# Two decay masks moved from PSUM to the factors they multiply, and block-diagonal gates packed onto four quarters of TensorE

## The chip, the cores and the metric

The kernel runs on one core of a Trainium2 chip. The metric is the device time of one execution in microseconds (us). A core has five engines with a queue each: TensorE (PE, with its weight loads shown apart as PEld), VectorE (DVE), ScalarE (ACT), GpSimd (POOL) and SyncE (SP), which issues nearly all transfers. Each engine works through its queue in order and waits, at an instruction, for what that instruction needs.

## What is computed

Two layers run over 256 positions of width 1024. The first has a Mamba-2 mixer, a gated linear recurrence (RG-LRU) and a gated feed-forward part; the second has four branches, one of them a gated delta net. The change touches three places of this:

```python
# first layer, SSD: decay between positions l >= s of a chunk, per head
seg   = a_cs[..., :, None] - a_cs[..., None, :]
decay = exp(where(causal, seg, -inf))
cb    = einsum("bclgn,bcsgn->bgcls", cc, bc)
y_diag = einsum("bgcls,bgecls,bcsgep->bclgep", cb, decay, xdt)

# first layer, RG-LRU: 16 blocks of 64 channels, two gates
xc = causal_dwconv(u_x, conv_w, conv_b)
xb = xc.reshape(b, s, 16, 64)
r = sigmoid(einsum("bshi,hij->bshj", xb, wr) + br)
i = sigmoid(einsum("bshi,hij->bshj", xb, wi) + bi)

# second layer, delta net: decay of a chunk, per head
L    = where(strict, (kb @ k.T) * exp(where(strict, diff, 0)), 0)
a_qk = where(incl,   (q  @ k.T) * exp(where(incl,   diff, 0)), 0)
```

## The kernel before

The large products (projections) set the length of the program. A weight is loaded in halves of 128 x 1024 numbers (`wraw`, three buffers, transfers on SP's queue), rounded by ACT (L112, `whi`) and its remainder taken by DVE (L113, `wlo`), five buffers each. A projection is three products of rounded parts, 128-row weights against 256 or 512 columns of positions. `z0` to `z3` and `lx0` to `lx3` are made by `proj_wide` (L468, then an ACT copy L471 and a DVE sum L472), the gates `g0` to `g3` and the outputs `pa`, `pb` of the two mixers by L430 to L432.

Everything else of a layer is written as generators beside the main loop: `side_ssd`, `side_lru`, `side_gn` (the norm of the SSD's output, which makes `YAH`, `YAL`, the input of `pa`), `side_decay`, `side_delta`. At each stop of a projection the main loop runs one of them up to its next `yield`, and so PE's order is fixed by where these stops fall. The queues of ACT, DVE, POOL and SP are put in order by a scheduler from estimated times.

**SSD.** During `z` and `lx`, `decay(h)` makes, for each of 16 heads, a PSUM tile `pe` of 384 columns: the running sum `csT` of the head broadcast over the rows (L719), and on its first 256 columns a large negative number above the diagonal, added by a product of the identity with `low2r` (L721). Three Exp on ACT (L723, L725, L726) give `M`, DVE multiplies it by the block products `CB` (L727). After every second head PE multiplies `M` by `XD` (`py`, L737); PE's queue holds `py` of heads 2t and 2t+1 ahead of the projection that goes on.

**RG-LRU.** `lx` of a pair p goes through a convolution over positions (ACT L607, then three DVE steps L610 for each of two tiles) into `XC`. `side_lru` then takes one 128-channel tile after another, eight in all: two float32 products of a 128 x 128 block-diagonal weight (two 64 x 64 blocks, zeros beside them) with 256 columns, one per gate, both in one PSUM bank `pg`, and two Sigmoids on ACT (L789, L790). The weights `lw` are 1 MB.

**Delta net.** `side_decay` makes per chunk c a bank `pdE` of 4 heads x 128 columns: the mask product (L1189, 512 columns), four broadcasts of the running sum (L1192), four Exp (L1196). DVE multiplies the result `EE` into the products `pkk` (L1295, L1300).

Of the kernel before, what the change touches and what calls it, by code (L numbers as in the profile page):

```python
# [11 lines left out]
ALU = mybir.AluOpType  # L12
# [184 lines left out]
def two_blocks_kernel(  # L197
# [113 lines left out]
    low2r = cp.tile([P, 2 * P], F32R, name="low2r")  # L311
# [7 lines left out]
    def constants():  # L319
# [22 lines left out]

        for i in range(2):
            nc.vector.tensor_scalar(low2r[:, i * P : (i + 1) * P], triu, -NEG, NEG,
                                    op0=ALU.mult, op1=ALU.add)
# [42 lines left out]
    def rows(o, src, nm, wait):  # L388

# [11 lines left out]
        w = o.shape[1] - S  # L401
        nc.vector.tensor_copy(o[:, w : w + S], pT[:, 0:S])
        if w:
            nc.vector.tensor_copy(o[:, 0:P], pT[:, P:S])
# [250 lines left out]
    lw = big.tile([P, 2, 8, P], F32, tag="lw", name="lw")  # L655
# [6 lines left out]
    csT = sm.tile([P, 384], F32R, name="csT", bufs=1)  # L662
    ncs = sm.tile([P, 32], F32, name="ncs", bufs=1)
    ncb = sm.tile([P, 16], F32, name="ncb", bufs=1)

    def side_dt():
# [19 lines left out]
        nc.vector.tensor_scalar(ncs, cs[:, 0:32], -1.0, None, op0=ALU.mult)  # L686
# [15 lines left out]
    def side_ssd():  # L702

        yield ("bc", 9)
        for g in range(2):
# [6 lines left out]
            nc.vector.tensor_copy(CB[:, g, :], pb[:, 0:384])  # L712
            yield 1
# [62 lines left out]
    GY = act8("b8", "GY")  # L776
    LA = act8("b5", "LA")
# [1109 lines left out]
```

## Time and profile before

| | before |
|---|---|
| median of 3 runs | 826.16 us (826.12 to 826.82) |
| the profiled execution's own time | 825.72 us |
| its span in the profile | 824.0 us |
| PE busy | 809.6 us (98%) |
| DVE busy | 612.2 us (74%) |
| ACT busy | 524.6 us (64%) |
| POOL busy | 61.0 us (7%) |

The span is the time between the first and the last instruction that the profiler recorded; 1.7 us of the execution lie outside it. A busy share is a mean over the whole program: PE is full nearly everywhere, ACT is full in some stretches and idle in others.

### The profile page before, as it was taken

Reading aid. Unit: us, or ns where it says so; the run is one execution under the profiler, and the core shown is the slowest. Engines: PE = TensorE matmul, PEld = TensorE weight load, DVE = VectorE, ACT = ScalarE, POOL = GpSimd, SP = SyncE. Lnnn points to the kernel's source line nnn. Section 1 sums busy time; section 2 is a strip of 40 time slices with the busy share of each in tenths; the row PEclk is TensorE's granted clock in tenths of the full one; section 3 lists DMA queues with packets and bytes.
Section 4 is the critical chain, followed back from the end, with each engine's and each line's share of the span. In section 5 each row is a group of like instructions: output and inputs, shape, how many; then the busy total and the mean of one; then the engine's idle time right before and its main releaser. Section 6 shows DMA issues by size and latency. Waiting matters only on the chain.

```text
span 824.0 us, 13302 instructions
## 1 busy us (share of the span) xinstructions
PE 809.6 (98%) x5060; PEld 721.0 (87%) x5060; DVE 612.2 (74%) x1026; ACT 524.6 (64%) x820; POOL 61.0 (7%) x101
## 2 busy tenths in 40 slices
PE   6999999999999999999999999999999999999997
PEld 6999888888889999999988889888888888888886
DVE  5989789889689788888744697877786647566583
ACT  7575988895656666565643478956976555544452
POOL 0000000000110000000000100028830000000000
PEclk9999999999999999999999999999999999999999
DMA  8545435556754655555555544542454344555551
GB/s 310 204 172 212 153 104 207 177 205 201 257 186 149 216 189 185 182 177 191 201 196 193 192 158 151 182 157 104 169 156 149 130 143 167 202 190 192 190 193 52
DMA packets 41248, 147.12 MB, mean 179 GB/s; under 512 B 4896, under 2 KB 5152, under 8 KB 41056
## 3 DMA queue, kind: packets, MB, share of 16 engines
q1 hardware_dynamic: 40464, 145.35, 51.1%
q0 software_dynamic: 576, 0.92, 0.5%
q8 instruction: 40, 0.66, 0.3%
q14 instruction: 24, 0.20, 0.1%
q10 hardware_dynamic: 144, 0.00, 0.0%
HBM read 144.94 MB, written 1.31 MB: 177 GB/s over the span
## 4 chain that ended last, share of the span: by engine, by line
PE 92%; DVE 5%; ACT 1%; DMA 1%; issue 1%; DVEq 0%; SPq 0%; ACTq 0%
PE z L468 8%; PE fu L432 6%; PE fu L431 6%; PE fu L430 6%; PE g L430 5%; PE g L432 5%; PE g L431 5%; PE lx L468 3%; PE fd L431 3%; PE fd L432 3%; PE fd L430 3%; PE up L430 2%; PE up L431 2%; PE up L432 2%; PE o L432 2%; PE o L430 2%
## 5 line engine op out<-in xcount | busy, mean ns | idle before, releaser
L113 DVE TENSOR_TENSOR wlo<-wraw,whi 128x1024 fp32r<-128x1024 f32 x256 | 311.9, 1226 | 131.6 <-ACT whi L112 130.1
L112 ACT CAST whi<-wraw 128x1024 fp32r<-128x1024 f32 x256 | 266.3, 1049 | 198.4 <-PE fu L431 48.0
L430 PE MATMUL fu<-HX,whi 128*128 128x256 f32 x384 | 108.7, 283 | 0.0
L431 PE MATMUL fu<-HX,whi 128*128 128x256 f32 x384 | 108.7, 283 | 0.0
L432 PE MATMUL fu<-HX,wlo 128*128 128x256 f32 x384 | 108.7, 283 | 0.0
L430 PE MATMUL g<-whi,HX 128*128 128x512 f32 x192 | 76.7, 399 | 0.0
L432 PE MATMUL g<-whi,HX 128*128 128x512 f32 x192 | 74.9, 390 | 0.0
L431 PE MATMUL g<-wlo,HX 128*128 128x512 f32 x192 | 74.8, 390 | 0.0
L430 PEld LDWEIGHTS fu<-HX,whi 128*128 128x128 f32 x384 | 73.7, 192 | 0.0
L431 PEld LDWEIGHTS fu<-HX,whi 128*128 128x128 f32 x384 | 73.7, 192 | 0.0
L432 PEld LDWEIGHTS fu<-HX,wlo 128*128 128x128 f32 x384 | 73.7, 192 | 0.0
L468 PE MATMUL z<-HX,whi 128*128 128x512 f32 x192 | 70.1, 402 | 0.0
L468 PE MATMUL z<-HX,wlo 128*128 128x256 f32 x192 | 51.0, 286 | 0.0
L610 DVE SCALAR_TENSOR_TENSOR fc<-fu,pc,fc 128x255 f32<-128x255 f32 (+1 forms) x96 | 43.8, 478 | 1.6
L432 PEld LDWEIGHTS g<-whi,HX 128*128 128x128 f32 x192 | 36.0, 188 | 7.7
L431 PEld LDWEIGHTS g<-wlo,HX 128*128 128x128 f32 x192 | 36.1, 188 | 7.2
L430 PEld LDWEIGHTS g<-whi,HX 128*128 128x128 f32 x192 | 36.1, 188 | 7.2
L431 PE MATMUL fd<-wlo,FH 128*128 128x512 f32 (+1 forms) x120 | 41.7, 347 | 0.0
L430 PE MATMUL fd<-whi,FH 128*128 128x512 f32 (+1 forms) x120 | 41.6, 347 | 0.0
L432 PE MATMUL fd<-whi,FL 128*128 128x512 f32 (+1 forms) x120 | 41.6, 347 | 0.0
L468 PEld LDWEIGHTS z<-HX,whi 128*128 128x128 f32 x192 | 35.5, 188 | 6.8 <-issue 0.9
L468 PEld LDWEIGHTS z<-HX,wlo 128*128 128x128 f32 x192 | 36.2, 189 | 1.5
(539 smaller groups left out, 1922.7 us busy)
## 6 DMA issues: line engine op xcount, KB each, us to landing
wraw<-in_w_in_dram SPq DMA_DIRECT2D x130, 512.0 KB, 3.8
wraw<-in_w_fu_dram SPq DMA_DIRECT2D x48, 512.0 KB, 3.8
wraw<-in_w_fd_dram SPq DMA_DIRECT2D x24, 512.0 KB, 3.7
wraw<-in_w_o_dram SPq DMA_DIRECT2D x16, 512.0 KB, 3.5
wraw<-in_w_up_dram SPq DMA_DIRECT2D x16, 512.0 KB, 3.4
wraw<-in_w_pa_dram SPq DMA_DIRECT2D x8, 512.0 KB, 3.6
wraw<-in_w_pb_dram SPq DMA_DIRECT2D x8, 512.0 KB, 4.4
wraw<-in_w_mk_dram SPq DMA_DIRECT2D x4, 512.0 KB, 4.1
```

The source lines that it names most:

```text
L112: nc.scalar.copy(hi, raw)
L113: nc.vector.tensor_tensor(out=lo, in0=raw, in1=hi.bitcast(F32), op=ALU.subtract)
L430: nc.tensor.matmul(o, wh, xh, start=first, stop=False)
L431: nc.tensor.matmul(o, wh, xl, start=False, stop=False)
L432: nc.tensor.matmul(o, wl, xh, start=False, stop=last)
L468: nc.tensor.matmul(*p, start=k + i == 0, stop=k == 7 and i == 1)
L610: nc.vector.scalar_tensor_tensor(o[:, d:S], in0=p[:, 0 : S - d], scalar=col(wname, (taps - 1 - d) * n + i), in1=o[:, d:S], op0=ALU.mult, o ...
```

## The change

1. **SSD decay.** `pe` keeps only the broadcast running sum, 256 columns wide (`csT` is 256 wide instead of 384), and the mask product and `low2r` are gone. On ACT, two Relu of 128 columns give max(cs - csT, 0), that is minus the decay's exponent where it is allowed and zero above the diagonal; one Exp over 256 columns of `M` itself follows, and the third Exp reads `pe` as before. What stands above the diagonal is now a finite number, and POOL sets the same places of `CB` to zero, once per group (`affine_select`).
2. **LRU gates.** Two tiles (a pair p) are taken at once. Eight products with 64 rows and 64 columns of weights: gate r uses `XC`, with block 0 on rows and columns 0 to 63 and block 1 on 64 to 127; gate i uses `XW`, a copy of `XC` with its two halves of 64 partitions swapped, on the two other quarters. Gate r has one PSUM bank for both tiles and gate i another. `XW` is filled by two transfers per pair of 64 partitions x 512 numbers (128 KB), issued on POOL's queue after the convolution's last step; the gates wait for them. `lw` is 512 KB, there are four stops of `side_lru` instead of eight, and each comes at the sixth tick after its `lx` event instead of the fifth.
3. **Delta net decay.** The mask product is gone; four Relu and one Exp of 512 columns take the place of four Exp, and POOL zeroes `EE` above the diagonal before DVE reads it.

```diff
-            nc.tensor.matmul(pe[:, 0:384], sel16[:, h : h + 1].to_broadcast([P, P]), csT,
-                             start=True, stop=False)
-            nc.tensor.matmul(pe[:, 0:256], identr, low2r, start=False, stop=True)
+            nc.tensor.matmul(pe[:, 0:S], sel16[:, h : h + 1].to_broadcast([P, P]), csT,
+                             start=True, stop=True)
             M = tmp(f"M{h}", 384, tag="pt", bufs=4)
-            nc.scalar.activation(
-                M[:, 0:128], pe[:, 0:128], AF.Exp, bias=ncs[:, 16 + h : 17 + h])
-            nc.scalar.activation(M[:, 128:256], pe[:, 128:256], AF.Exp, bias=ncs[:, h : h + 1])
-            nc.scalar.activation(M[:, 256:384], pe[:, 256:384], AF.Exp, bias=ncb[:, h : h + 1])
+            for b in range(2):
+                nc.scalar.activation(M[:, (1 - b) * P : (2 - b) * P], pe[:, b * P : (b + 1) * P],
+                                     AF.Relu, scale=-1.0, bias=cs[:, 16 * b + h : 16 * b + h + 1])
+            nc.scalar.activation(M[:, 0:256], M[:, 0:256], AF.Exp, scale=-1.0)
+            nc.scalar.activation(M[:, 256:384], pe[:, P:S], AF.Exp, bias=ncb[:, h : h + 1])
...
+            v = CB[:, g, 0:256].rearrange("p (b l) -> p b l", b=2)
+            nc.gpsimd.affine_select(out=v, in_=v, compare_op=ALU.is_ge, fill=0.0, base=0,
+                                    pattern=[[0, 2], [1, P]], channel_multiplier=-1)
...
-        for i in range(8):
-            yield (f"lx{i // 2}", 5)
-            pg = bank(f"pg{i}")
-            for a in range(2):
-                nc.tensor.matmul(pg[:, a * S : (a + 1) * S], lw[:, a, i, :], XC[:, i, :],
-                                 start=True, stop=True)
+        for p in range(4):
+            yield (f"lx{p}", 6)
+            two = [bank(f"pg{p}{a}") for a in range(2)]
+            for j in range(2):
+                i = 2 * p + j
+                for r in range(2):
+                    for a, src in enumerate((XC, XW)):
+                        k = slice(64 * r, 64 * r + 64)
+                        m = k if a == 0 else slice(64 - 64 * r, P - 64 * r)
+                        nc.tensor.matmul(two[a][m, j * S : (j + 1) * S], lw[k, a, i, :],
+                                         src[k, i, :], start=True, stop=True)
...
             conv([XC[:, i, :] for i in two], ps, "lru_conv_w", two, 8, 4, "lru_conv_b")
+            for r in range(2):
+                nc.gpsimd.dma_start(XW[64 * r : 64 * r + 64, 2 * p : 2 * p + 2, :],
+                                    XC[64 - 64 * r : P - 64 * r, 2 * p : 2 * p + 2, :])
...
-                nc.tensor.matmul(v4(pe), identr, low2r[:, 0:P].unsqueeze(1).to_broadcast(
-                    [P, 4, P]), start=True, stop=False)
...
                 for h in range(4):
-                    nc.scalar.activation(EE[c][:, h, :], pe[:, h * P : (h + 1) * P], AF.Exp,
-                                         bias=ngc[:, 4 * c + h : 4 * c + h + 1])
+                    nc.scalar.activation(EE[c][:, h, :], pe[:, h * P : (h + 1) * P], AF.Relu,
+                                         scale=-1.0, bias=gc[:, 4 * c + h : 4 * c + h + 1])
+                nc.scalar.activation(EE[c], EE[c], AF.Exp, scale=-1.0)
+                nc.gpsimd.affine_select(
+                    out=EE[c], in_=EE[c], compare_op=ALU.is_ge, fill=0.0, base=0,
+                    pattern=[[0, 4], [1, P]], channel_multiplier=-1)
```

ACT's queue in the SSD stretch, from the weight cast ahead of head 10 (`M_1364` before, `M_1360` after) on. `SZ` is the Silu of z's first half for `side_gn`, with a load of its function table ahead of it and one of the Exp table behind it. Before:

```order
L112 CAST whi_1346<-wraw_1250 128x1024
L841 ACT_TABLE_LOAD
L841 ACTIVATE SZ<-SZ 128x1024
L723 ACT_TABLE_LOAD
L723 ACTIVATE M_1364<-pe_1361,ncs 128x128
L725 ACTIVATE M_1364<-pe_1361,ncs 128x128
L726 ACTIVATE M_1364<-pe_1361,ncb 128x128
L723 ACTIVATE M_1380<-pe_1377,ncs 128x128
```

Now:

```order
L112 CAST whi_1343<-wraw_1247 128x1024
L715 ACTIVATE M_1360<-pe_1358,cs 128x128 x2
L718 ACTIVATE M_1360<-pe_1358,ncb 128x128
L717 ACTIVATE M_1360<-M_1360 128x256
L715 ACTIVATE M_1376<-pe_1374,cs 128x128 x2
L718 ACTIVATE M_1376<-pe_1374,ncb 128x128
L717 ACTIVATE M_1376<-M_1376 128x256
L460 COPY lx_s<-lx_0_1347 128x256
L843 ACT_TABLE_LOAD
L843 ACTIVATE SZ<-SZ 128x1024
L715 ACTIVATE M_1400<-pe_1398,cs 128x128 x2
L718 ACT_TABLE_LOAD
```

The Silu with its two loads moved two heads back. Before, it was the second such group among the 16 heads (the other stood between heads 3 and 4); now it is the only one, and the other Silu stands behind head 15, ahead of the convolution of `lx1`.

DVE's queue at the end of the convolution of `lx1` (L610 before, L599 now; the `XC` tiles 2 and 3). Before:

```order
L610 SCALAR_TENSOR_TENSOR XC<-lx_s,pc,XC 128x255 x2
L610 SCALAR_TENSOR_TENSOR XC<-lx_s,pc,XC 128x254 x2
L610 SCALAR_TENSOR_TENSOR XC<-lx_s,pc,XC 128x253 x2
L113 TENSOR_TENSOR wlo_1531<-wraw_1441,whi_1530 128x1024
L113 TENSOR_TENSOR wlo_1537<-wraw_1447,whi_1536 128x1024
L113 TENSOR_TENSOR wlo_1603<-wraw_1528,whi_1602 128x1024
L472 TENSOR_TENSOR lx_s<-lx_0_1540,lx_s 128x256
```

Now:

```order
L599 SCALAR_TENSOR_TENSOR XC<-lx_s,pc,XC 128x253
L599 SCALAR_TENSOR_TENSOR XC<-lx_s,pc,XC 128x254
L113 TENSOR_TENSOR wlo_1538<-wraw_1446,whi_1537 128x1024
L113 TENSOR_TENSOR wlo_1606<-wraw_1529,whi_1605 128x1024
L113 TENSOR_TENSOR wlo_1612<-wraw_1535,whi_1611 128x1024
L599 SCALAR_TENSOR_TENSOR XC<-lx_s,pc,XC 128x253
L461 TENSOR_TENSOR lx_s<-lx_0_1541,lx_s 128x256
```

The last of the six steps, after which POOL issues the two transfers of `XW`, now stands behind three weight remainders. On PE's queue the gates of pairs 0, 1 and 2 stand where `pg` of tiles 0, 1 and 2 stood, and those of pair 3 stand 24 `g` products behind pair 2.

DVE's queue at the end of `side_gn`. `YAL` is made in four pieces, of which `pa` reads the last two from its 25th product on. Before:

```order
L873 SCALAR_TENSOR_TENSOR XS<-XS,pc,pgr 128x256 x3
L113 TENSOR_TENSOR wlo_1856<-wraw_1785,whi_1855 128x1024
L354 TENSOR_TENSOR YAL<-XS,YAH 128x512 x2
L113 TENSOR_TENSOR wlo_1862<-wraw_1791,whi_1861 128x1024
L354 TENSOR_TENSOR YAL<-XS,YAH 128x512
L804 SCALAR_TENSOR_TENSOR IB<-IB,RB 128x1024
```

Now:

```order
L825 TENSOR_TENSOR GY<-GY,RB 128x1024 x2
L113 TENSOR_TENSOR wlo_2045<-wraw_2000,whi_2044 128x1024
L113 TENSOR_TENSOR wlo_2075<-wraw_2036,whi_2074 128x1024
L113 TENSOR_TENSOR wlo_2081<-wraw_2042,whi_2080 128x1024
L1032 TENSOR_TENSOR G_1697<-g_00_2034,gb_1693 128x512
L349 TENSOR_TENSOR YBL<-GY,YBH 128x1024 x2
L1032 TENSOR_TENSOR G_1697<-g_10_2035,gb_1693 128x512
L113 TENSOR_TENSOR wlo_2118<-wraw_2072,whi_2117 128x1024
L113 TENSOR_TENSOR wlo_2124<-wraw_2078,whi_2123 128x1024
L349 TENSOR_TENSOR YAL<-XS,YAH 128x512 x2
```

The last two pieces of `YAL` moved from the middle of the `g` projections to behind the whole recurrence (`GY`, `YBL`) and the first weights of `pa`.

## Rows read from the trace of the kernel before

**Rows 1.** The page's busy times and the chain that ended last, whole program.

```profile
PE 809.6 (98%) x5060; PEld 721.0 (87%) x5060; DVE 612.2 (74%) x1026; ACT 524.6 (64%) x820; POOL 61.0 (7%) x101
...
PE 92%; DVE 5%; ACT 1%; DMA 1%; issue 1%; DVEq 0%; SPq 0%; ACTq 0%
```

**Rows 2.** Timeline of PE, one head's decay: start us, duration us, what, shapes.

```profile
95.60 0.34 PE L719 MATMUL pe<-csT,sel 128*128 128x384 f32 x1
95.78 0.28 PE L721 MATMUL pe<-low2r,ident2r 128*128 128x256 f32 x1
95.90 0.28 PE L468 MATMUL z<-HX,wlo 128*128 128x256 f32 x1
```

**Rows 3.** Timeline of ACT in the SSD stretch; in brackets the idle time before.

```profile
100.49 0.37 ACT L723 ACTIVATE M<-pe,ncs 128x128 f32<-128x128 f32 x1 [0.47 <-PE pe L721]
...
101.25 1.05 ACT L112 CAST whi<-wraw 128x1024 fp32r<-128x1024 f32 x1
...
104.32 1.28 ACT L841 ACT_TABLE_LOAD   x1
...
107.98 0.37 ACT L723 ACTIVATE M<-pe,ncs 128x128 f32<-128x128 f32 x1
```

**Rows 4.** Timeline of ACT, two functions over 256 columns one behind the other.

```profile
157.91 0.47 ACT L789 ACTIVATE RB<-pg,pc 128x256 f32<-128x256 f32 x1
158.28 0.47 ACT L790 ACTIVATE IB<-pg,pc 128x256 f32<-128x256 f32 x1
```

**Rows 5.** Timelines of DVE and PE: `M` of heads 1 and 13, and its readers.

```profile
87.97 0.56 DVE L727 TENSOR_TENSOR M<-M,bBC 128x384 f32<-128x384 f32 x1 [0.16 <-ACT M L726]
...
88.91 0.87 PE L737 MATMUL py<-M,XD 128*64 128x256 f32 x8
...
113.94 0.56 DVE L727 TENSOR_TENSOR M<-M,bBC 128x384 f32<-128x384 f32 x1
...
115.26 0.87 PE L737 MATMUL py<-M,XD 128*64 128x256 f32 x8
```

**Rows 6.** Timeline of PE, the gates of one tile inside a `g` projection.

```profile
153.40 1.02 PE L787 MATMUL pg<-XC,lw 128*128 128x256 f32 x4
...
154.49 0.40 PE L431 MATMUL g<-wlo,HX 128*128 128x512 f32 x1
```

**Rows 7.** Timeline of PE, products on halves of the array (columns, then rows).

```profile
97.68 0.87 PE L737 MATMUL py<-M,XD 128*64 128x256 f32 x8
...
98.82 0.40 PE L468 MATMUL z<-HX,wlo 128*128 128x256 f32 x2
...
569.09 0.93 PE L1466 MATMUL psc<-bM,bGS 64*128 64x128 f32 x8
```

**Rows 8.** Timelines of DVE and PE around the gates of tiles 1 and 2.

```profile
125.47 1.22 DVE L113 TENSOR_TENSOR wlo<-wraw,whi 128x1024 fp32r<-128x1024 f32 x1 [0.36 <-ACT whi L112]
...
130.64 1.02 PE L787 MATMUL pg<-XC,lw 128*128 128x256 f32 x4
...
134.29 1.02 PE L787 MATMUL pg<-XC,lw 128*128 128x256 f32 x4
```

**Rows 9.** Transfers on POOL's queue (KB each, median us to landing) and POOL's timeline.

```profile
bXY<-dl POOLq DMA_DIRECT2D x4, 128.0 KB, 5.2
...
bXY<-dx POOLq DMA_DIRECT2D x4, 32.0 KB, 2.0
...
546.40 2.48 POOL L1215 DMA_DIRECT2D dl<-bLA  x4 [61.91 <-DVE bLA L1295]
```

**Rows 10.** The delta net's mask product, and DVE's first read of the decay.

```profile
L1189 PE MATMUL pdE<-low2r,ident2r x2: 387/387/387, 532.7 to 535.6; 128*128 128x512 f32 x2
...
538.01 0.60 DVE L1295 SCALAR_TENSOR_TENSOR bLA<-pkk,wk,bLA 128x128 f32<-128x128 f32 x2
```

**Rows 11.** Timeline of PE at the 26th and 27th product of `pa`.

```profile
189.45 0.39 PE L431 MATMUL pa<-wlo,YAH 128*128 128x512 f32 x1
189.68 0.39 PE L432 MATMUL pa<-whi,YAL 128*128 128x512 f32 x1
```

More of the change, by code (lines that the diff above doesn't have):

```diff
@@ L310, in two_blocks_kernel @@
     triu = cp.tile([P, P], F32, name="triu")
-    low2r = cp.tile([P, 2 * P], F32R, name="low2r")
     sel16 = cp.tile([P, 16], F32R, name="sel16")
@@ L341, in constants @@
                                     op=ALU.add)
-        for i in range(2):
-            nc.vector.tensor_scalar(low2r[:, i * P : (i + 1) * P], triu, -NEG, NEG,
-                                    op0=ALU.mult, op1=ALU.add)
         for i in (0, 2):
@@ L400, in rows @@
             nc.tensor.transpose(pT[:, tt * P : (tt + 1) * P], cat[:, tt].bitcast(F32), ident)
[L401 to L404, printed above, removed]
+        nc.vector.tensor_copy(o, pT[:, 0:S])
     def softplus(o, v, n, nm):
@@ L654, in two_blocks_kernel @@
     nsp8 = cp.tile([P, 8], F32, name="nsp8")
-    lw = big.tile([P, 2, 8, P], F32, tag="lw", name="lw")
+    lw = big.tile([P, 2, 8, 64], F32, tag="lw", name="lw")
     dtab, baab = [], []
@@ L661, in two_blocks_kernel @@
     cs = sm.tile([P, 48], F32, name="cs", bufs=1)
-    csT = sm.tile([P, 384], F32R, name="csT", bufs=1)
-    ncs = sm.tile([P, 32], F32, name="ncs", bufs=1)
+    csT = sm.tile([P, S], F32R, name="csT", bufs=1)
     ncb = sm.tile([P, 16], F32, name="ncb", bufs=1)
@@ L685, in side_dt @@
         yield from rows(csT, cs[:, 0:32].rearrange("p (t h) -> p t h", t=2), "pcT", 5)
-        nc.vector.tensor_scalar(ncs, cs[:, 0:32], -1.0, None, op0=ALU.mult)
         nc.vector.tensor_tensor(out=ncb, in0=cs[:, 32:48], in1=cs[:, 0:16], op=ALU.subtract)
@@ L776, in two_blocks_kernel @@
     GY = act8("b8", "GY")
+    XW = act8("b5", "XW")
     LA = act8("b5", "LA")
@@ L782, in side_lru @@
         W.first = True
-        for i in range(8):
-            yield (f"lx{i // 2}", 5)
-            pg = bank(f"pg{i}")
-            for a in range(2):
-                nc.tensor.matmul(pg[:, a * S : (a + 1) * S], lw[:, a, i, :], XC[:, i, :],
-                                 start=True, stop=True)
-            nc.scalar.activation(RB[:, i, :], pg[:, 0:S], AF.Sigmoid, bias=col("lru_br", i))
-            nc.scalar.activation(IB[:, i, :], pg[:, S : 2 * S], AF.Sigmoid,
-                                 bias=col("lru_bi", i))
+        for p in range(4):
[9 more added lines that the diff above has]
+                                         src[k, i, :], start=True, stop=True)
+            for o, ps, b in zip((RB, IB), two, ("lru_br", "lru_bi")):
+                for j in range(2):
+                    i = 2 * p + j
+                    nc.scalar.activation(o[:, i, :], ps[:, j * S : (j + 1) * S], AF.Sigmoid,
+                                         bias=col(b, i))
             yield 1
@@ L1178, in side_decay @@
             gcT = sm.tile([P, S], F32R, name="gcT", bufs=1)
-            ngc = sm.tile([P, 8], F32, name="ngc", bufs=1)
-            nc.vector.tensor_scalar(ngc, gc[:, 0:8], -1.0, None, op0=ALU.mult)
             nc.vector.tensor_tensor(out=kds, in0=gc[:, 8:12], in1=gc[:, 0:4], op=ALU.subtract)
@@ L1193, in side_decay @@
                                      sel4[:, h : h + 1].to_broadcast([P, P]),
-                                     gcT[:, c * P : (c + 1) * P], start=False, stop=h == 3)
+                                     gcT[:, c * P : (c + 1) * P], start=True, stop=True)
                 for h in range(4):
-                    nc.scalar.activation(EE[c][:, h, :], pe[:, h * P : (h + 1) * P], AF.Exp,
-                                         bias=ngc[:, 4 * c + h : 4 * c + h + 1])
+                    nc.scalar.activation(EE[c][:, h, :], pe[:, h * P : (h + 1) * P], AF.Relu,
[4 more added lines that the diff above has]
+                    pattern=[[0, 4], [1, P]], channel_multiplier=-1)
                 yield 1
@@ L1845, in _layout @@
     ).reshape(P, 8 * 24)
-    lw = np.zeros((P, 2, 8, P), np.float32)
-    for i, name in enumerate(("lru_wr", "lru_wi")):
-        v = a(name)[0]
-        for t in range(8):
-            lw[0:64, i, t, 0:64] = v[2 * t]
-            lw[64:128, i, t, 64:128] = v[2 * t + 1]
-    d["lruw"] = lw.reshape(P, 2 * 8 * P)
+    lw = [a(name)[0].reshape(8, 2, 64, 64) for name in ("lru_wr", "lru_wi")]
+    lw = np.stack([lw[0], lw[1][:, ::-1]])
+    d["lruw"] = lw.transpose(2, 3, 0, 1, 4).reshape(P, 2 * 8 * 64)
     d["wsT"] = np.ascontiguousarray(a("spatial_w_2")[0].transpose(2, 0, 1)).reshape(P, 4 * P)
```

## The prediction

> **What bounds the kernel now.** I read the busy times first, then the chain of work that ended last, and then the timelines of the stretches that the change touches. PE is busy for 98% of the span and is 92% of the chain [rows 1], and in the touched stretches its products follow one another without a gap: a product taken off PE's queue there is worth its own step, and nothing else in the program can pay. The other half of the question is whether the engines that feed PE keep up once PE is earlier, or are themselves later. That is read from the distance between the end of a feeding step and the start of its reader on PE, and it is small: head 13's `M` is done at 114.50 and `py` begins at 115.26 [rows 5].
>
> **SSD, what PE saves.** Steps, not durations, count, since products overlap. L719 takes 95.78 - 95.60 = 0.18 us and L721 0.12 [rows 2]; a broadcast of 256 columns instead takes the 0.12 of a 256-column product. Each of 16 heads gives back 0.18, together **-2.9 us**, if PE never waits. `low2r`, one copy of `csT` and the negated sums also go; DVE made them where nobody waited for them, so they count for nothing.
>
> **SSD, what ACT pays.** Three Exp of 128 columns take 101.25 - 100.49 = 0.76 us, 0.25 each [rows 3]. After the change there are three operations of 128 columns and one of 256. A 256-column function steps by 158.28 - 157.91 = 0.37 [rows 4], so a head costs 1.12 and 16 heads cost 5.8 us more. In return one of the two groups load, Silu, load leaves the stretch, which is 107.98 - 104.32 = 3.66 us [rows 3]. By head 15 ACT is behind by 5.8 - 3.7 = 2.1 us, less the little idle time that it had (0.47 in rows 3): about 1.6, while PE would like to be 2.9 earlier. No table is loaded between Relu and Exp, as the queue printed above shows.
>
> Where this hits PE follows from the slots of `py`. *Head 1:* its three Exp wait behind head 0's, so both heads are 0.36 longer; `M` is ready at 88.53 + 0.7 = 89.2 [rows 5], while PE, with four decays already shortened, comes to `py` at 88.91 - 0.7 = 88.2. PE waits 1.0. *Heads 3 to 11:* with the first Silu group gone ACT is ahead again, no wait. *Head 13:* the Silu group now stands just ahead of head 12; 14 heads cost 5.0 more and 3.66 less, minus 0.47 idle: `M` is done at 114.50 + 0.9 = 115.4. PE comes at 115.26 - 2.9 + 1.0 = 113.4. PE waits 2.0. *Head 15* has the slack of the wait before it. Waits: **+3.0 us**. The SSD part as a whole comes out at +0.1; if a Relu steps by less than an Exp, or the 256-column operation by less than 0.37, at most 1.5 of the waits go, and a chain of Relu and Exp on the same tile that pays a delay for each could add 1.
>
> **POOL's zeroing of `CB`** is done long before head 0 reads it and is taken at nothing; POOL is idle there.
>
> **LRU, what PE saves.** One tile's gates push the projection back by 154.49 - 153.40 - 0.23 = 0.86 us [rows 6] (0.23 is the step of a 512-column product, 189.68 - 189.45 [rows 11]): four passes of 0.215, as float32 takes two passes. Eight tiles: 6.9. Four quarters at once do not occur in this trace. The nearest are two halves at once: in `py` the column halves start in pairs [rows 7] and the eight records cost 98.82 - 97.68 - 0.23 = 0.91, of which the columns, counted once per pair, need 0.65; with 0.09 ahead of the group the change of tiling costs about 0.35. If four quarters run together, a pair of tiles streams 4 x 0.215 and costs 0.86 + 0.35 = 1.21, four pairs 4.8: **-2.0 us**. If only two run together, a pair costs 1.72 + 0.35 = 2.07. I take the first, as column halves and row halves (`psc`) each overlap fully.
>
> **LRU, what PE waits for.** The gates now need `XW`, so a transfer stands between the convolution and PE, for which the two conditions (last DVE step, landing) have to be timed.
>
> *The convolution of pair 1.* Its last step moved behind three remainders, the last of which was 125.47 to 126.6 [rows 8]. The Silu that now stands behind head 15, with its load 3.66 - 1.28 = 2.4 us, is ahead of this convolution and of those casts, so the third remainder ends at about 128.7 and the step at 129.1. *Pair 2.* Between this step and pair 2's last one DVE's queue holds, by the steps of these operations, two sums of `lx` (0.7), two of `SZ` and two of `gnsq` (1.9), five convolution steps before the last and the last (2.4), one remainder (1.1) and another sum (0.3): 6.4 us without idle time, so it ends at 135.5.
>
> *The transfers.* POOL issues one in 2.48 / 4 = 0.6 us [rows 9], so the second of a pair starts 0.7 after the step. On this queue 32 KB landed in 2.0 us and 128 KB in 5.2 [rows 9]. The latter has the size of `XW`'s, but moves many short pieces into 32 partitions; `XW`'s rows are 2 KB in one piece over 64 partitions. I take 2.0 to 2.6, nearer to the quick row, and keep 5.2 for the range. The Trainium skill, "DMA: Bandwidth & Descriptors", section "Anatomy of one DMA — SWDGE (gpsimd) path", fits such a transfer by a fixed 2.0 us plus its bytes over 436 GB/s, an estimate of 2.3 us for 128 KB; the 5.2 us row does not agree with it, the 2.0 us row does. By it the sum below would stay within 0.3 us of what it is.
>
> *PE's slots.* Pair 1 stands at 130.64 and pair 2 at 134.29 [rows 8], each pushed back by 0.35 for every pair ahead of it: 131.0 and 135.0. `XW` of pair 1 is there at 131.8 to 132.4, that of pair 2 at 138.2 to 138.8. The second wait covers the first: PE has lost 3.2 to 3.8 when pair 2 is through, **+3.5 us**. Pair 3 comes 24 products later (5.4 us), its `XW` some 6 us after pair 2's: no further wait of note. The gates' products after it find everything there. The LRU part: +1.5.
>
> **Behind it.** The last two pieces of `YAL` now end late on DVE's queue. Its remainders wait for buffers that PE frees, so it cannot run far ahead; by the steps of the queue the third piece ends some 0.5 to 1 us before PE wants it at 189.68 [rows 11]. I take nothing, with 1.5 as the price if DVE is later.
>
> **Delta net.** Two products of 512 columns go, 2 x 0.23 = **-0.45 us** [rows 10, 11]. ACT's extra Exp and POOL's zeroing of 512 columns put the first L1295 back by 1 to 2 us from 538.01 [rows 10]; behind it are only products of the delta net whose next use waits for POOL's transfers at 546.40 [rows 9], so PE is not held, and if it were the price is up to 1.
>
> **The sum.** -2.9 + 3.0 - 2.0 + 3.5 - 0.45 = +1.15 on the profiled execution's 825.72 us, that is 826.9. The median of the runs stands 0.44 above that execution, so the figure to compare with 826.16 is 827.3; I round down to 827.2. Its own range is 825.2 to 829.0.
>
> **Rivals.**
>
> *PE alone decides.* The waits that I add are walks along two queues by hand; if ACT and DVE have more room than I gave them (the idle time in their rows taken up, shorter Relu, `XW` landed in time), PE keeps 2.9 + 2.0 + 0.45 = 5.3 us, 820.8; with half of the waits, 824. For it speaks the 98% of PE; against it that `M` is 0.4 and 0.8 us ahead of its reader already [rows 5].
>
> *Slow transfers.* If 128 KB lands in 5.2 us as in rows 9, pair 2 has its `XW` at 141.4 and PE loses 6.4 instead of 3.5: 830.1, slower. It decides from a landing time of some 3.2 us on.
>
> *Two quarters at a time.* In this kernel the row halves of `psc` go to two banks and the column halves of `py` share one with all rows in use [rows 7]; the change has both row halves writing one bank at different partitions, which no row shows. If the second row half then waits for the first, pairs 2 and 3 cost 0.86 more each (those of pairs 0 and 1 vanish in the wait that follows): 828.9, slower. The Trainium skill, "TensorEngine Tiling (Array Packing)", section "Restrictions and Gotchas", says that different row tiles cannot access the same PSUM bank at one time, which speaks for this rival; no row of before can show whether it holds at different partitions.
>
> **How the numbers follow.** A measurement of this kernel tells 0.2%, 1.65 us, from no change: faster is below 824.5, slower above 827.8. Chances: my sum 0.42, PE alone (fully or in part) 0.29, slow transfers 0.13, two quarters 0.16. Of the 0.42, 0.03 lies below 824.5, 0.27 between and 0.12 above; two quarters give 0.03 to no change. Faster 0.32, same 0.30, slower 0.38. The range leaves out the full saving's lower end and the worst of the transfers: 821.8 to 830.8.
>
> **What would show it.** Right: in the changed kernel PE's idle time stands ahead of `py` of heads 1 and 13, released by DVE's `M`, and ahead of the gates of pairs 1 and 2, released by the transfers of `XW`; ACT is full from 86 to 116 us; the four products of a quarter set start within some 10 ns. Wrong: no idle time ahead of `py` (ACT's Relu are cheaper than I took them), `XW` landed before PE comes, or the gates' products in two steps of two. A wait that I don't name, ahead of the `YAL` products of `pa` above all, would make the time longer than all of these.

## The result: 1.1% slower

The changed kernel takes 834.94 us (median; 834.36 to 837.66) beside 826.14 us for the kernel before on the same chip: ratio 1.0112, interval 1.0089 to 1.0135. The forecast was 827.2, range 821.8 to 830.8, so the time lies outside it. The profiled execution took 834.90 us, with a span of 833.1; that of before had 824.0, so 9.1 us have to be found.

The busy lines and the shares of the chain of the changed kernel answer to [rows 1]. PE's busy time has hardly changed; what grew is the chain's share of DVE, ACT and DMA, at PE's cost.

```profile
PE 808.6 (97%) x5074; PEld 715.7 (86%) x5074; DVE 612.1 (73%) x1021; ACT 524.7 (63%) x834; POOL 67.5 (8%) x113
...
PE 83%; DVE 7%; ACT 4%; DMA 3%; issue 2%; DVEq 0%; SPq 0%; ACTq 0%
```

PE's products come in the same order but for the edits, so the start of one product in both traces says how far PE is behind at that place:

| place on PE | before, us | after, us | behind by |
|---|---|---|---|
| first `pcb` (C B blocks, ahead of SSD) | 58.28 | 60.34 | +2.06 |
| last `py` (end of SSD) | 119.67 | 121.72 | +2.05 |
| first `g` product (two pairs of gates behind it) | 132.90 | 144.11 | +11.21 |
| first `pa` product (all gates behind it) | 183.78 | 192.61 | +8.83 |
| last `pa` product | 205.32 | 214.86 | +9.55 |
| first `pkk` (behind the delta net's decays) | 536.21 | 545.36 | +9.15 |
| end of the span | 824.00 | 833.14 | +9.14 |

Four terms come out of it: 2.06 ahead of everything that was predicted, 0.0 for the SSD part, 6.7 for the gates (8.83 less the 2.13 that PE was behind at the first of them), and 0.7 at the `YAL` products of `pa`; the delta net gives 0.4 back.

**The start-up, +2.06.** `pcb` waits for ACT's Silu of `bBC`. Timelines of ACT, of the kernel before and then of after, from the last step of the dt softplus to that Silu:

```profile
55.86 0.21 ACT L412 ACTIVATE splam_e<-splam_ab 128x8 f32<-128x8 f32 x1 [1.14 <-DVE spdt_q L424]
56.30 1.28 ACT L994 ACT_TABLE_LOAD   x1 [0.23 <-DVE bBC L610]
57.59 0.63 ACT L994 ACTIVATE bBC<-bBC 128x512 f32<-128x512 f32 x1
```

```profile
57.14 0.21 ACT L401 ACTIVATE splam_e<-splam_ab 128x8 f32<-128x8 f32 x1 [1.88 <-DVE spdt_q L413]
57.30 1.05 ACT L112 CAST whi<-wraw 128x1024 fp32r<-128x1024 f32 x1
58.37 1.28 ACT L996 ACT_TABLE_LOAD   x1
59.66 0.63 ACT L996 ACTIVATE bBC<-bBC 128x512 f32<-128x512 f32 x1
```

The softplus ends 1.28 us later, and a weight cast of 1.05 us now stands between it and the table load. No line of the diff is near: the scheduler has put the engines' start-up work in another order. Why is tested below.

**SSD, 0.0.** Timeline of PE at heads 1 and 13, where `M` comes late:

```profile
90.24 0.65 PE L729 MATMUL py<-M,XD 128*64 128x256 f32 x2
91.21 0.86 PE L729 MATMUL py<-M,XD 128*64 128x256 f32 x6 [0.33 <-DVE M L719]
...
95.24 0.87 PE L729 MATMUL py<-M,XD 128*64 128x256 f32 x8
...
99.25 0.87 PE L729 MATMUL py<-M,XD 128*64 128x256 f32 x8
...
115.35 0.65 PE L729 MATMUL py<-M,XD 128*64 128x256 f32 x2
117.30 0.86 PE L729 MATMUL py<-M,XD 128*64 128x256 f32 x6 [1.31 <-DVE M L719]
...
121.12 0.87 PE L729 MATMUL py<-M,XD 128*64 128x256 f32 x8
```

Between two groups without a wait PE steps 99.25 - 95.24 = 4.01 us for two heads; before it was 97.68 - 93.30 = 4.38. That is 0.18 for each head, the whole saving. The steps with a wait are 95.24 - 90.24 = 5.00, a wait of 0.99, and 121.12 - 115.35 = 5.77 against 119.07 - 115.26 = 3.81 before, a wait of 1.96. (The bracket shows less, since it counts from the modelled end of a product.) Saved and waited cancel.

**The gates, +6.7.** Timeline of PE at the first two pairs. The four products of a set start within 20 ns. From the `lx` product at 128.79 to the next of its shape at 130.35 there are 1.56 us, less the 0.35 that two `lx` products take without a pair (130.35 to 130.70): pair 0 costs 1.21, as forecast.

```profile
128.79 0.39 PE L457 MATMUL lx<-HX,whi 128*128 128x512 f32 x1
129.11 0.43 PE L787 MATMUL pg<-XC,lw 64*64 64x256 f32 x1
129.12 0.43 PE L787 MATMUL pg<-XW,lw 64*64 64x256 f32 x1
129.12 0.43 PE L787 MATMUL pg<-XC,lw 64*64 64x256 f32 x1
129.13 0.43 PE L787 MATMUL pg<-XW,lw 64*64 64x256 f32 x1
...
130.13 0.39 PE L457 MATMUL lx<-HX,wlo 128*128 128x256 f32 x1
130.35 0.39 PE L457 MATMUL lx<-HX,whi 128*128 128x512 f32 x1
...
130.70 0.40 PE L457 MATMUL lx<-HX,whi 128*128 128x512 f32 x1
...
133.14 0.64 PE L787 MATMUL pg<-XC,lw 64*64 64x256 f32 x2
139.50 0.66 PE L787 MATMUL pg<-XW,lw 64*64 64x256 f32 x1 [5.72 <-DMA XW<-XC]
...
141.50 0.58 PE L457 MATMUL lx<-HX,wlo 128*128 128x256 f32 x1
```

At pair 1 PE stands for 5.72 us, released by the transfer of `XW` (6.09 between the starts of the two products on either side; waits below are given as such distances). Of the pieces of the chain there, as start, length and what, one is a long transfer (the DVE step ahead of it is the last one of pair 1's convolution):

```profile
130.68 0.39 DVE XC L599
...
131.62 7.75 DMA XW<-XC
139.37 0.14 issue
139.50 2.07 PE pg L787 x14
```

128 KB took 7.75 us, though the median of the eight transfers is 2.6. SP's timeline (its DMA queue) says what was under way: three weight tiles of 512 KB, issued at 128.43, 129.56 and 130.70, and the bias `gb`, also 512 KB, at 131.08. They landed at 131.77, 134.14, 137.32 and 138.75; `XW`, issued at 131.62, landed behind all of them, at 139.37.

```profile
118.80 12.23 SPq L87 DMA_DIRECT2D wraw<-in_w_in_dram  x6
131.08 0.43 SPq L1021 DMA_DIRECT2D gb<-in_gbias_dram  x1
```

The view by stretches shows what such a wait costs beyond its length. Columns: stretch and length, busy time of PE, PEld, DVE, ACT and POOL, then PE's granted clock, the share of the DMA engines' time, and GB/s.

```profile
126.00:134.00 8.00, 7.78 (x53) 5.65 (x51) 8.00 (x15) 7.48 (x11) 1.03 (x2) 1.00 0.61 190
134.00:136.00 2.00, 0.00 (x0) 0.00 (x0) 1.38 (x2) 2.00 (x5) 0.00 (x0) 1.00 0.98 344
136.00:138.00 2.00, 0.00 (x0) 0.00 (x0) 2.00 (x6) 0.08 (x1) 0.00 (x0) 0.78 1.01 299
138.00:140.00 2.00, 0.50 (x6) 0.53 (x10) 0.68 (x3) 0.00 (x0) 1.03 (x2) 0.50 0.52 182
140.00:142.00 2.00, 2.00 (x16) 1.18 (x9) 0.00 (x0) 0.49 (x2) 0.00 (x0) 0.50 0.43 107
142.00:144.00 2.00, 2.00 (x8) 1.71 (x8) 0.40 (x2) 1.56 (x4) 0.00 (x0) 0.51 0.00 0
144.00:146.00 2.00, 2.00 (x16) 1.35 (x18) 1.35 (x4) 1.32 (x2) 0.00 (x0) 1.00 0.00 0
```

The DMA engines are full from 134 to 138. PE's granted clock falls while PE stands (0.78, then 0.50, the lower level, 1.2 of 2.4 GHz) and is back at 1.00 from 144 on, 4.5 us after PE resumed. At 0.50 pair 1 takes 141.50 - 139.50 = 2.00 where pair 0 took 130.13 - 129.11 = 1.02, and eight `lx` products take 144.11 - 141.50 = 2.61 instead of four steps of 0.35: 2.2 us in all. The 9.08 us (11.21 - 2.13) between the first gate and the first `g` product are 5.9 of waiting (6.09 less a step), two pairs put in for two tiles (2 x 0.35 = 0.7), 2.2 of slow clock, and 0.3 that I don't assign. Pairs 2 and 3 then return 2.4 (8.83 - 11.21): four quarters in place of whole products. Pair 2 has no wait of note: PE comes to it at 145.67, and its `XW`, issued at 138.70 and 139.21, landed at 141.45 and 141.65.

**`YAL`, +0.7.** Timelines of PE and DVE at `pa`: a remainder of 1.23 us has got in front of the third and fourth pieces of `YAL`, and PE waits for them.

```profile
199.09 0.50 PE L421 MATMUL pa<-whi,YAL 128*128 128x512 f32 x1 [0.43 <-DVE YAL L349]
...
197.21 1.23 DVE L113 TENSOR_TENSOR wlo<-wraw,whi 128x1024 fp32r<-128x1024 f32 x1 [0.17 <-ACT whi L112]
198.35 1.29 DVE L349 TENSOR_TENSOR YAL<-XS,YAH 128x512 fp32r<-128x512 f32 x2
```

### The profile page after: what moved, and what is told of

Same layout as the page of the kernel before. It is cut to its first block, busy times and chain, and to the rows that moved or that the text cites. A ratio compares the mean times of both kernels' runs of the same rounds, so it can differ in the third digit from the quotient of the medians.

```text
span 833.1 us, 13389 instructions
## 1 busy us (share of the span) xinstructions
PE 808.6 (97%) x5074; PEld 715.7 (86%) x5074; DVE 612.1 (73%) x1021; ACT 524.7 (63%) x834; POOL 67.5 (8%) x113
## 4 chain that ended last, share of the span: by engine, by line
PE 83%; DVE 7%; ACT 4%; DMA 3%; issue 2%; DVEq 0%; SPq 0%; ACTq 0%
PE z L457 8%; PE fu L419 6%; PE fu L420 6%; PE fu L421 6%; PE g L419 4%; PE g L421 4%; PE g L420 4%; PE fd L420 3%; PE fd L419 3%; PE fd L421 3%; DVE wlo L113 2%; PE up L421 2%; PE up L419 2%; PE up L420 2%; PE o L421 2%
## 5 line engine op out<-in xcount | busy, mean ns | idle before, releaser
L599 DVE SCALAR_TENSOR_TENSOR fc<-fu,pc,fc 128x255 f32<-128x255 f32 (+1 forms) x96 | 43.8, 479 | 1.6
```

Source lines behind the costliest of these rows:

```text
L599: nc.vector.scalar_tensor_tensor(o[:, d:S], in0=p[:, 0 : S - d], scalar=col(wname, (taps - 1 - d) * n + i), in1=o[:, d:S], op0=ALU.mult, o ...
```

## The experiments

| kernel | edit | median, us (before on the same chip) | ratio, interval |
|---|---|---|---|
| e1_old_gates | changed kernel with the old gates | 827.41 (826.61) | 1.0008, 0.9999 to 1.0017 |
| e2_gates_only | before with the new gates alone | 834.50 (826.61) | 1.0095, 1.0078 to 1.0112 |
| e3_bias_early | one bias load moved ahead | 832.80 (826.61) | 1.0073, 1.0056 to 1.0091 |
| e5_keep_low2r | the two unused DVE steps kept | 831.61 (826.61) | 1.0057, 1.0042 to 1.0072 |
| e4_xw_act | `XW` issued by ACT | 835.05 (826.26) | 1.0109, 1.0090 to 1.0127 |
| e15_read_xc | PE doesn't wait for `XW` | 828.55 (826.26) | 1.0034, 1.0022 to 1.0046 |
| e9_old_gates_keep | SSD and delta net alone, start-up as before | 826.02 (826.70) | 0.9990, 0.9981 to 1.0000 |
| e7_clip_dve | the clip on DVE, old gates | 832.21 (826.70) | 1.0067, 1.0052 to 1.0082 |
| e6_shift | no `XW`, ACT writes across | 832.14 (826.70) | 1.0064, 1.0049 to 1.0079 |
| e8_clip_shift | both of these | 837.63 (826.70) | 1.0133, 1.0116 to 1.0150 |
| e11_tail_later | changed kernel, `YAL` later | 834.56 (826.43) | 1.0105, 1.0090 to 1.0121 |
| e13_shift_later | e6_shift, `YAL` later | 827.24 (826.43) | 1.0009, 1.0000 to 1.0018 |
| e12_three_repairs | e3, e5 and e11 in one | 830.25 (826.43) | 1.0047, 1.0034 to 1.0061 |
| e10_best | new gates as in e13, delta net, old SSD | 827.28 (826.43) | 1.0011, 1.0002 to 1.0020 |
| e14_pair3_later | e10 with pair 3 one step later | 827.83 (826.26) | 1.0014, 1.0005 to 1.0023 |

**Which part loses: e1_old_gates and e2_gates_only.** The first takes the changed kernel and puts back the old gates (`lw`, `side_lru` and no `XW`); the second puts the new ones into the kernel before.

> The changed kernel with the gates of before (eight tiles, block-diagonal weights, no XW). Theory A, three separate losses, by the traces: an order of the queues that reaches PE at pcb (+2.06 us at 60 us), the wait for XW of pair 1 with the slow clock behind it (+9.1 between the first gates and the first g product), and the late YAL at pa (+0.7), with the SSD part even (0.0) and the delta net -0.43. By it this kernel keeps the first and the delta net alone: 826.1 + 2.1 - 0.4 = 827.8, SSD even from z to the last py. Rival B, ACT's extra work in the SSD part is what runs through to the end: above 831, with PE waiting at py and behind it.

> The kernel before with the change's gates alone (XW by transfers on the POOL queue, four quarters); masks as before. Theory A: no wait at pcb, a wait of several us for XW of pair 1 with the lower clock behind it, four groups of gates of 1.2 us instead of eight of 0.86: 826.1 - 2.0 + 5 to 8 = 829 to 832. Rival B (ACT's work in the SSD part): 824.1, as there is none of it here and XW is in time.

Without the new gates nearly all of the loss is gone (1.0008 for 1.0112), though `pcb` is still 1.92 late: the SSD part is again 0.0, the delta net gives 0.45, `pa` waits for nothing. The gates alone cost 8 us. In e2 the loads lie elsewhere in time, and so does the wait: pair 1 has its `XW` in time, and pair 2 waits twice, once for each of its two transfers.

```profile
139.94 0.61 PE L795 MATMUL pg<-XW,lw 64*64 64x256 f32 x1 [3.82 <-DMA XW<-XC]
...
142.67 0.69 PE L795 MATMUL pg<-XW,lw 64*64 64x256 f32 x1 [1.62 <-DMA XW<-XC]
```

The first wait, 4.20, ends with a quick transfer: the convolution's last step ends at 137.06, the transfer is issued at 137.61 and lands at 139.80, 2.19 later. That is the wait that was forecast for pair 2 (3.2 to 3.8). The second, 2.25, is for a transfer issued at 138.12, beside a weight load of 138.22, that lands at 142.62, after 4.50. Behind them PE's granted clock is 0.50 from 140 to 146 us. So the new transfer has two costs, a late convolution and a landing beside weights, and the place in the program decides which of them holds PE.

**The cause of the late transfer: e3_bias_early, e4_xw_act, e15_read_xc.** One reading is that the sixteen DMA engines are shared, and `XW` comes behind the loads issued earlier. The other is that POOL's queue itself is held up, by DVE's work for instance. The first test takes one of these loads, the bias, away; the second issues the same transfers on ACT; the third leaves all transfers but lets PE read `XC` in their place (the second kind's gates then see the halves unswapped).

```diff
-            if p == 3:
-                gb = [big.tile(...) for n in range(2)]
+            if p in (0, 3):                     # e3: gb[0] at lx0, gb[1] at lx3
+                n = p // 3
...
-                nc.gpsimd.dma_start(XW[...], XC[...])
+                nc.scalar.dma_start(XW[...], XC[...])      # e4
...
-                    for a, src in enumerate((XC, XW)):
+                    for a, src in enumerate((XC, XC)):     # e15
```

> The changed kernel with the transfer of the first gate bias (512 KB, issued 0.5 us ahead of XW of pair 1) moved to the event lx0, some 25 us earlier; nothing else stands in another order. Theory C, XW of pair 1 lands late (7.7 us) since it shares the transfer engines with 1.5 MB issued in the 3 us ahead of it: a third of that is gone, it lands in about 5 us, PE waits 2.5 to 3.5 instead of 5.9 and little or nothing is lost to the clock: 829 to 830.5. Rival D, transfers of POOL's queue are held up by what DVE does (it was busy up to 138.67, and XW landed at 139.1): no change, 834.9.

> The changed kernel with the transfers of XW issued on ACT's queue instead of POOL's. Theory C, they wait behind the weights and the bias on the same transfer engines: the pair that is issued within 3 us behind them still takes 5 us or more to land. Rival D, transfers that POOL issues are held up by DVE's work: on ACT's queue every one lands in 2 to 3 us. The time itself says less, since ACT now waits for the convolutions and the order of its queue differs.

> The changed kernel with PE reading XC in the places where it reads XW, so the second gate is taken from the wrong half of the channels; the transfers of XW are still issued and land as before, only nothing on PE waits for them. Theory C, the wait for XW and the slow clock behind it are the loss at the gates: PE goes through pair 1 at about 133 us, the clock stays full, 834.9 - 5.9 - 2.3 - a small rest = 826 to 827. Rival Q, the convolutions or the casts behind them are late as well and take the place of the transfer: 829 or more.

The last line of the view of tile `XW`, issue to landing in us as least, median and most, for e3 and then for e4:

```profile
DMA to landing us min/median/max: 2.2/2.4/5.5
```

```profile
DMA to landing us min/median/max: 2.2/3.3/5.4
```

With the bias out of the way the worst landing falls from 7.75 to 5.46, as expected, PE waits 3.81, and 2.1 us of the median come back (its four runs lie between 831.5 and 834.7). The time expected, 829 to 830.5, was missed: the shorter wait, too, brought PE's granted clock down (0.55 and 0.60 in the two stretches from 138 to 142 us), and the wait at `YAL` was 1.08 (0.81 in the changed kernel). On ACT's queue (two runs) the transfers are late as well wherever they meet loads: pair 1 took 4.6 and 5.4, with one load on its way and three more issued within 2.7 us, pair 2 4.4 and 4.2 behind a load issued 0.5 us ahead, pairs 0 and 3 2.2 to 2.4. (Of the 5.76 that PE waits at pair 2 there, 1.25 passed before the transfer was issued.) So POOL's queue is not what holds them up; the engines are shared, and they are full while `XW` is late. In e15 the transfers take up to 7.1 us all the same, but PE's one wait at the gates is for a convolution, 0.62 by starts:

```profile
PE pg L787 <- DVE XC L599: 0.2, 1, 0.2
```

Its granted clock stays at 1.00, PE is only 0.61 behind at the first `pa`, and the time falls by 6.4. Part is paid again at `pa` (waits of 1.91 for `YAH` and 0.75 for `YAL`).

**The start-up: e5_keep_low2r.** The two DVE steps that built `low2r` are put back, though nothing reads them.

```diff
+    low2r = cp.tile([P, 2 * P], F32R, name="low2r")
...
+        for i in range(2):
+            nc.vector.tensor_scalar(low2r[:, i * P : (i + 1) * P], triu, -NEG, NEG,
+                                    op0=ALU.mult, op1=ALU.add)
```

> The changed kernel with the two DVE operations that made low2r put back; nothing reads it. The queues of ACT, DVE and SP up to 80 us are in the order of before again. Theory E, the 2.06 us at pcb come from the order alone, which the scheduler built anew when these two operations went: 834.9 - 2.1 = 832.8, pcb at 58.3. Rival F, they come from the change itself (csT, CB, POOL's zeroing): 834.9, pcb at 60.3.

The view of tile `pcb` in e5, with the first and last start at the end, against 60.3 to 62.8 in the changed kernel:

```profile
L701 PE MATMUL pcb<-bBC x4: 377/380/483, 58.3 to 60.7; 128*128 128x256 f32 x4
```

With two more steps of work `pcb` is back at 58.31 and the kernel is 3.3 us faster: 2.0 of start-up, and a transfer that meets the loads a little better (6.6 us, wait 4.98). So the removal of two steps that "DVE made where nobody waited" changed the scheduler's order from the start on, to the worse. How much that is worth, one pair of profiles tells only roughly, since `pcb` scatters with the order the same: in the six profiles without the two steps it starts at 59.73 to 60.34, in the eleven with them (that of before among them) at 57.98 to 59.39. The groups don't overlap, and their means are 1.3 us apart; e1 and e9, which differ in these two steps alone, have ratios of 1.0008 and 0.9990, 1.5 us apart. The other 0.7 of the 2.06 would then be scatter.

**SSD by itself: e9_old_gates_keep and e7_clip_dve.** e9 is e5 with the old gates. e7 does the clip on DVE instead of ACT, since ACT's extra work makes `M` late (at head 13 not alone: in the changed kernel ACT is done with it at 116.04, and DVE takes its step at 116.69, behind five steps of the convolution):

```diff
-                nc.scalar.activation(M[...], pe[...], AF.Relu, scale=-1.0, bias=cs[...])
+                nc.vector.tensor_scalar(M[...], pe[...], cs[...], 0.0,
+                                        op0=ALU.subtract, op1=ALU.min)
```

> The change's two decay parts alone (SSD and delta net), gates of before, and the two DVE operations that made low2r kept so that the queues up to 80 us are in the order of before. Theory G, the SSD part is even (2.9 us of products gone, 2.9 of waits for M in their place, at py of heads 1 and 13) and only the delta net counts: 826.1 - 0.4 = 825.7, the last py at 119.7 as before. Rival H, the waits come from the order at 50 to 80 us and not from ACT: 823.

> The kernel of e9_old_gates_keep with the two Relu of a head replaced by two DVE operations (subtract cs, then the smaller of that and zero), so that ACT has one Exp of 256 and one of 128 columns per head instead of four operations. Theory G, ACT's work is what makes PE wait for M: with it 0.14 us under before per head PE keeps most of its 2.9: 822.5 to 824. Rival I, DVE then is the one that is late (two operations of about 0.25 us for 16 heads are 8 us, and DVE is 70 to 75% busy there): 826 to 830, with PE waiting for M as before or longer.

e9 gives 0.9990: SSD even, the delta net's 0.45 kept, the waits of heads 1 and 13 still there. In e7 the waits move from ACT to DVE. The waits of PE (total, times, longest) and the stretch 108 to 122 us:

```profile
PE py L736 <- DVE M L726: 4.5, 4, 1.6
PE py L736 <- ACT M L725: 0.9, 1, 0.9
```

```profile
108.00:122.00 14.00, 11.60 (x70) 8.70 (x70) 13.20 (x32) 7.31 (x19) 0.00 (x0) 1.00 0.38 120
```

In the same stretch of before DVE was busy for 11.98 and ACT for 13.00. The clip relieves ACT to 7.31 and fills DVE to 13.20 of 14; SSD loses 6 us, more than either theory had. Neither of the two places for the clip keeps the saving on PE; one Relu on each engine wasn't tried.

**Four quarters without a transfer: e6_shift, e8_clip_shift.** Both kinds read `XC`, each half of the array on its own rows, and ACT writes the second kind's Sigmoid to the other half's partitions, 64 partitions at a time. e8 adds e7's clip.

```diff
-                    for a, src in enumerate((XC, XW)):
+                    for a, src in enumerate((XC, XC)):
...
+                for r in range(2):
+                    k, m = slice(64 * r, 64 * r + 64), slice(64 - 64 * r, P - 64 * r)
+                    nc.scalar.activation(IB[k, i, :], two[1][m, j * S : (j + 1) * S],
+                                         AF.Sigmoid, bias=col("lru_bi", i)[k])
```

> The kernel of e5_keep_low2r with gates that need no XW: both kinds read XC, gate i comes out on the other half of the partitions, and ACT's Sigmoid writes it back to its own half (four operations of 64 partitions instead of two of 128 per pair). Theory A, all that the gates lost was the transfer and what follows from it: 826.1 - 0.4 - 2.0 = 823.7, up to 0.7 more if YAL is late; each pair 1.2 us on PE, the clock full. Rival J, the four quarters or ACT's eight more Sigmoids (0.37 us each) hold PE as well: 826 or more, with PE waiting for casts behind them.

> e6_shift and e7_clip_dve together: the change's three parts with the Relu on DVE and no transfer. Theories A and G: the two gains add, 826.1 - 0.4 - 2.0 - 2.0 to 2.9 = 820.8 to 821.7. Rivals I and J: DVE's 32 more operations delay the convolutions and the remainders behind them, 824 or more.

PE's waits in e6 from the gates to `pa`:

```profile
PE pa L426 <- DVE YAL L354: 3.0, 1, 3.0
PE pg L791 <- DVE XC L604: 1.8, 2, 1.3
```

The transfer's wait is gone. At the gates PE loses 0.1 net, since it now catches up with the convolutions themselves. But at `pa` it loses 5.6 to `YAL`, partly at a granted clock of 0.89 (184 to 200 us). In e8 the losses of e6 and e7 add up.

**`YAL`: e11_tail_later, e13_shift_later, e12_three_repairs.** In the new `side_lru` four pairs hand over one step each where eight tiles did, so the recurrence behind them enters the queues earlier. One line hands it over later:

```diff
             yield 1
+        yield 6
         for hf in range(2):
```

> The changed kernel with the recurrence behind the gates handed to the queues six ticks later, so that the four pieces of YAL stand on DVE where they stood before, ahead of GY and YBL. Theory L, the late YAL costs what PE waited at pa (0.8 us idle, 0.7 between the first and the last pa): 834.9 - 0.7 = 834.2, no idle time at pa. Rival M, YAL's wait only takes the place of another (the weights of pa): 834.9.

> e6_shift with the recurrence handed over six ticks later. In e6_shift PE lost 5.6 us between the first and the last pa, idle ahead of YAL and slow behind it. Theory L: all of this is the place of YAL on DVE, 832.1 - 5.6 = 826.5 (826.1 - 0.4 for the delta net, the gates' 2.0 eaten by waits of 0.9 and 1.7 for the convolutions). Rival M: the gates without transfers keep ACT so busy that the casts for pa are late in any order: 830 or more.

> The changed kernel with three things put right that are not its arithmetic: the two DVE operations of low2r kept (order up to 80 us), the first gate bias loaded 25 us earlier, and the recurrence handed over six ticks later. Theory N, the losses are separate and add: 834.9 - 3.3 (as e5_keep_low2r) - 2.1 (as e3_bias_early) - 0.7 = 828.8, what is left being the wait for XW behind the weights. Rival O, they hide behind one another: 831 or more.

In e13 PE's waits in the same stretch as above are those for `XC` alone, 1.8 in all as in e6; the one for `YAL` is gone. With one line e6 goes from 832.14 to 827.24, and in e11 the first and the last `pa` are behind by the same 8.50; there the time itself moves no more than the runs scatter. The three repairs together (e12) bring the changed kernel to 830.25, where the sum of their gains would be 828.8, and it still waits 3.73 for an `XW` that takes 5.4 us.

**Can the quarters' gain be had: e10_best, e14_pair3_later.** The old SSD with its mask product, gates as in e13, pairs 2 and 3 handed over one step later so that their convolutions are done; e14 gives pair 3 one step more.

```diff
-            yield (f"lx{p}", 6)
+            yield (f"lx{p}", 6 if p < 2 else 7)        # e10
+            yield (f"lx{p}", (6, 6, 7, 8)[p])          # e14
```

> The kernel before with the delta net's change and with the gates on four quarters without transfers (XC for both kinds, ACT writes gate i back to its half), pairs 2 and 3 one tick later and the recurrence six ticks later; SSD as before. Theory P, without the transfer, and with each pair's convolution done before PE comes, the four quarters give their 2.0 us: 826.1 - 2.0 - 0.4 = 823.7, faster than both kernels. Rival J, ACT's eight more operations delay the casts and PE waits for them: 825 to 827.

> e10_best with the gates of pair 3 one more tick later (2.7 us), as PE waited 2.1 us there for its convolution. Theory P, the four quarters give their 2.0 us once every convolution is done before PE comes: 827.3 - 2.1 = 825.2, faster than both kernels by little. Rival R: what PE gains is given back at the transposes of the merged branches (0.97 and 1.60 us idle there in e10_best against 0.55 in the kernel before), where it waits for DVE: 827.

PE's waits of e14 from the gates to `m1b`:

```profile
PE pa L431 <- DVE wlo L113: 1.6, 1, 1.6
PE pgr L597 <- DVE gnrl L354: 1.5, 1, 1.5
PE m1b L958 <- DVE MG L1068: 1.0, 1, 1.0
PE pg L794 <- DVE XC L610: 0.4, 1, 0.4
```

In e10 the gates are 0.35 ahead in spite of a wait of 2.13 at pair 3, so the quarters are worth some 2.5 us; PE then waits 0.97 and 1.60 at `m1b`. In e14 the wait at pair 3 falls to 0.78, and 1.84 at `pgr` and 2.02 at `pa` stand in its place (this profile is of the longest of eleven runs, 825.55 to 828.56). Neither beats the kernel before, nor does any other version here by more than 0.2%. Behind the gates PE waits each time for a step of DVE; where it comes earlier, it waits longer there.

## Why the prediction was wrong

Right were: *SSD even* (forecast +0.1, measured 0.0, with waits of 0.99 and 1.96 at exactly the heads 1 and 13, forecast 1.0 and 2.0); *the delta net* (-0.43 for -0.45); *four quarters together* (sets of four within 20 ns, 1.21 for a pair); *the convolutions of pairs 1 and 2* (done at 131.07 and 138.14; the forecast, moved by the 2.06 of the start-up, 131.2 and 137.6). The rival of two quarters at a time has fallen with that. The Trainium skill, "TensorEngine Tiling (Array Packing)", section "Restrictions and Gotchas", says that different row tiles cannot access one PSUM bank at the same time; here two row halves wrote one bank at different partitions at 129.11 to 129.13 without a delay, so for that arrangement the measurement decides against it. One reading was wrong without a cost: "No table is loaded between Relu and Exp"; at heads 0 and 12 the Exp table is loaded just there (87.25 and 111.74), in place of ahead of the head.

Wrong were four steps. The step that failed is the price of PE's wait for `XW`, *"+3.5 us"*: measured were 8.1, of which 5.9 are waiting and 2.2 slow clock (steps 1 and 2). The other two are terms that were put at nothing.

1. *"I take 2.0 to 2.6, nearer to the quick row."* The size of the transfer was priced, not its company. 2.2 us is right for a transfer that is alone; the one that decided took 7.75, beyond the range's end of 5.2. It made the wait 2.4 longer than forecast (5.9 for 3.5). Had it been quick, PE would have stood at pair 2 instead, as the prediction says; no run shows this kernel so, but in e15, where PE doesn't wait for `XW`, it comes to pair 2 at 136.72, and the transfers land at 140.43 and 141.75, and in e2 it waits there for 4.20. What would have told it stands in the trace of before: the DMA engines were 0.81 busy from 126 to 134 us (the line stands below), when pair 1's transfer would run, and 0.46 from 134 to 142. The place was off with it: pair 1, not pair 2, holds PE. The rival of slow transfers had the right direction, with 5.2 as its worst. The Trainium skill, "DMA: Bandwidth & Descriptors", section "Anatomy of one DMA — SWDGE (gpsimd) path", has a fit by which 128 KB are estimated at 2.3 us; the transfers that ran alone (2.2) agree, those among loads (4.2 to 7.9) don't.
2. *A wait was priced at its own length.* 5.9 us of waiting at the gates cost some 2.2 more, because PE's granted clock fell to 0.50 and stayed there until 144. I had no term for it. With the wait as short as forecast there would still have been one: behind the 3.81 of e3 the clock fell, too.
3. *"they count for nothing"*, of the removed DVE work. Their time does; their removal moved the scheduler's order ahead of 80 us, and with it `pcb`, by 2.06 in this profile and by about 1.3 on the mean of all (59.73 to 60.34 without the steps, 57.98 to 59.39 with them). I had compared the orders only around the places that the diff touches.
4. *`YAL` taken at nothing, price 1.5.* 0.7 in the changed kernel, 5.6 in e6.

The DMA engines in the kernel before, for step 1 (columns as above):

```profile
126.00:134.00 8.00, 8.00 (x44) 6.95 (x43) 7.72 (x14) 6.55 (x9) 0.00 (x0) 1.00 0.81 276
```

The sum by the forecast's terms with what was measured: SSD 0.0 instead of +0.1, LRU 6.7 instead of +1.5, delta net -0.43, `YAL` 0.7 instead of 0, start-up 2.06 instead of nothing: 9.0, of 9.1. Against the forecast of the profiled execution (826.9) that is a miss of 8.0: 2.4 of waiting, 2.2 of clock, 2.1 of start-up, 0.7 of `YAL`, and 0.6 of small rest. The wait with its clock, 4.6 over its forecast, is enough to leave the range; the longer transfer by itself, 2.4, is not.

What stays open: why the scheduler's order changes with two short steps, what the scatter of the start-up is, and whether `XW` could be had in time with the weights' loads held back; this wasn't tried.

## What to carry to other kernels

Price a new transfer by what else is in flight when it is issued: read the DMA share of that stretch in the trace before, and put ahead of it the loads that are issued shortly before. A wait put into a stream of products can cost more than its length, by the slow clock behind it (here 2.2 us behind 5.9), so a small saving on the busiest engine is only worth its waits if its feeders are ahead. And when a scheduler sets the order, compare the whole order from the first instruction on, not only around the edit.

## What the runs showed of the chip that I had not expected

- A transfer of 128 KB landed in 2.2 us alone, 4.2 to 4.5 with one load of 512 KB issued within 0.5 us of it (e4, on ACT's queue; e2, on POOL's), 5.2 to 5.5 with two loads still to land (e3, e12), and 6.6 to 7.9 with three (e5, e15, after, e11).
- After 6 us of idle time PE ran at a granted clock of 0.50 for 4.5 us more, at full load (140 to 144 us, 2.00 of 2.00 busy).
- Four products on four quarters of the array, two of them into one bank at different partitions, start within 20 ns; sets follow each other by 0.21 to 0.27 us, about the step of one whole product.
- ACT can write 64 partitions of PSUM to the other 64 of its target (e6, e10); eight tiles of it cost PE nothing at the gates but the wait for the convolutions.
